# A chunked RWKV-7 recurrence on one NeuronCore: each chunk's map of the state worked out beside the inverse

## The chip, the core and the metric

The kernel runs on one core of a Trainium2 chip. The metric is device time in microseconds (us) of one execution, the median of some runs. PE is TensorE, DVE is VectorE, ACT is ScalarE, POOL is GpSimd, SP is SyncE, whose queue issues the DMAs here. Each engine works through its own instructions in order. L1550 means line 1550 of the kernel before; lines of the changed kernel are named as such.

## What is computed

One layer of a hybrid encoder: one projection of the normalised input, three mixers (A: RWKV-7, B: forgetting attention, C: sparse attention with a top-k), gates, and an output projection, for a prompt of 1024 rows and a sample of 64. The change concerns A, which has 8 heads of 64 columns and a state S of 64x64 per head:

```python
def step(S, inp):
    r_t, w_t, k_t, v_t, kk_t, a_t = inp
    sa = jnp.einsum('bhij,bhj->bhi', S, -kk_t)
    S = (S * w_t[:, :, None, :] + sa[..., None] * (kk_t * a_t)[:, :, None, :]
         + v_t[..., None] * k_t[:, :, None, :])
    return S, jnp.einsum('bhij,bhj->bhi', S, r_t)
wkv, y = lax.scan(step, wkv0, (tm(r), tm(decay), tm(k), tm(v), tm(kk), tm(a)))
```

## The kernel before

**Chunks, slots, units.** The 1024 rows are cut into 16 chunks of 64 rows, the sample is one more. Within a chunk the recurrence is solved in closed form, which needs the inverse of a triangular 64x64 matrix; from chunk to chunk only S is carried. A slot is one chunk of a pair of heads (the two heads h lie on partitions 0 to 63 and 64 to 127), a unit is four slots: 4 pairs x 4 units of the prompt, and the sample of all four pairs, 17 units and 68 slots.

**The steps of a unit**, each a generator that yields between its parts: `prepare` (L1271: `elem` loads wt, zt and QR and works out decays and scaled rows; `chunk_rows` makes the rows BA and the matrices BN and ND), `chunk_invert` (L1476: five doubling levels in float16, a correction, and the inverse UD), `value_rows` (L1411: turns values into UV and multiplies them by BN into P1), `chain` (below), and `tail` (L1586: norm, gate, store).

**The chain** (L1520) goes through the four slots of a unit one after the other. For each it multiplies S by QR (L1545), adds P1 into za (L1546), multiplies by the inverse UD (L1550), copies the result into UV (L1555), multiplies UV by BA for the new state (L1558, L1563), and by BA and S by QR for the output (L1567, L1569). Each of these waits for the one ahead:

```python
nc.tensor.matmul(pa[hv[h]], QR[hv[h], c, 1], S[hv[h]], ...)            # L1545
v.tensor_tensor(za, pa, P1[:, c], op=OP.add)                           # L1546
nc.tensor.matmul(pb[hv[h]], UD[hv[h], c], za[hv[h]], ...)              # L1550
v.tensor_copy(UV[hv[h], h, c], pb[hv[h]])                              # L1555
nc.tensor.matmul(ch[hv[h], ...], BA[:, h, c, 64 * h:64 * h + 64], UV[:, h, c], ...)   # L1558
v.scalar_tensor_tensor(self.state, ch[...], Pt[:, c, 64:65], sp, ...)  # L1563
```

**What sets the order.** `braid` lays the steps of several units side by side: in turn u, the tail of unit u-2, the chain of u-1, the inverse and value rows of u, and the preparation of u+1, each step at a fraction of the turn (step k of n stands at (k+0.5)/n, value rows at 0.4 of that); the top-k of mixer C runs along on DVE and ACT. After every step `pump` adds R_A/10 of a credit, and each whole credit issues one step of filler: three matmuls (L154) of the projections of the other mixers, 24 steps per 128 columns. What is left of the filler goes into the attention stage at other rates; after its last step the weights of the output projection take its place in SBUF, and then the output products (L1683) are the filler. Behind this a scheduler settles each engine's order from the program's order, priorities and when buffers come free.

**Buffers.** zt, P1, UV and UD have two buffers, QR and BA three, since the chain of u-1 still reads what the preparation of u+1 doubles. PSUM has eight banks: two for projections, one for turns, and the rings ga (one, preparation), gb (two, inverse), gc and gd (one each, chain).

## Time and profile before

| | |
|---|---|
| time, median of 3 runs | 1339.45 us (1335.56 to 1340.52) |
| profiled execution | 1332.74 us, its span 1331.0 us |
| PE busy | 1264.6 us, 95% of the span |
| DVE, ACT, POOL busy | 64%, 58%, 50% |
| mean granted clock of PE | 0.979 of 2.4 GHz |
| RWKV stage (L1398 and its like) | about 182 to 762 us |
| attention B and C, output | about 762 to 1331 us |

Busy times are shares of the span; PE's matmuls are pipelined and their ends are modelled, so what PE can do more is read from the waits and from the distance between starts. A matmul of float32 stands in the trace as two records.

### The profile page before, as it was taken

How to read it: one execution, taken by the hardware profiler on the slowest of the kernel's cores; microseconds unless marked ns; L12 is line 12 of the kernel's file. 1: busy time of each engine (PE TensorE's matmuls, PEld its weight loads, DVE VectorE, ACT ScalarE, POOL GpSimd, SP SyncE). 2: the span in 40 equal slices, each digit the busy share in tenths (PEclk: the TensorE clock that was granted, in tenths of full speed). 3: DMA queues.
4: the chain of work that ended last, by engine and by line, in shares of the span. 5: the costliest groups of instructions: out<-in, count | busy, mean ns of one | idle time of the engine just before them, and what ended most of it. 6: DMA issues, size and time to landing. Idle time of an engine off the chain costs nothing.

```text
span 1331.0 us, 29369 instructions
## 1 busy us (share of the span) xinstructions
PE 1264.6 (95%) x10563; PEld 963.3 (72%) x10563; DVE 847.0 (64%) x2483; ACT 776.7 (58%) x1758; POOL 667.7 (50%) x975
## 2 busy tenths in 40 slices
...
GB/s 224 71 109 67 133 82 98 62 62 94 63 70 110 95 80 127 136 94 111 101 104 112 117 215 250 219 193 216 189 171 157 145 206 182 145 116 108 92 75 96
DMA packets 172621, 169.60 MB, mean 127 GB/s; under 512 B 38546, under 2 KB 147130, under 8 KB 172475
## 3 DMA queue, kind: packets, MB, share of 16 engines
...
HBM read 104.61 MB, written 62.24 MB: 125 GB/s over the span
## 4 chain that ended last, share of the span: by engine, by line
PE 75%; DVE 9%; DMA 8%; ACT 4%; issue 2%; SPq 1%; POOL 1%; DVEq 0%; POOLq 0%; ACTq 0%
PE pproj L154 33%; PE pproj L1683 7%; PE ps_pv L980 5%; PE ps_atp L107 5%; PE ps_tp L1683 4%; PE ps_ga L1398 3%; PE ps_sc L949 2%; DMA wraw<-in_w_in_dram 2%; PE ps_sc L950 2%; PE ps_gb L1457 2%; PE ps_gb L1464 1%; PE ps_tp L107 1%; ACT junka L588 1%; PE ps_gc L1567 1%; PE ps_gc L1558 1%
## 5 line engine op out<-in xcount | busy, mean ns | idle before, releaser
L154 PE MATMUL pproj<-uH,wh 128*128 128x384 f32 (+4 forms) x1088 | 493.7, 454 | 0.0
L154 PE MATMUL pproj<-uH,wl 128*128 128x384 f32 (+4 forms) x1088 | 363.3, 334 | 0.0
L154 PE MATMUL pproj<-uL,wb 128*128 128x384 bf16 (+4 forms) x1088 | 358.7, 330 | 0.4 <-DVE zg L770 0.4
L154 PEld LDWEIGHTS pproj<-uH,wh 128*128 128x128 f32 (+1 forms) x1088 | 217.2, 200 | 3.5 <-issue 0.4
L154 PEld LDWEIGHTS pproj<-uH,wl 128*128 128x128 f32 (+1 forms) x1088 | 207.7, 191 | 2.2 <-issue 0.2
L154 PEld LDWEIGHTS <-wb 128*128 128x128 bf16 (+1 forms) x1088 | 106.3, 98 | 116.6 <-issue 79.7
L588 ACT ACTIVATE junka<-score,tk_tau 128x1024 f16<-128x1024 f32 (+4 forms) x160 | 149.3, 933 | 44.0 <-DVE tk_tau L602 26.5
L901 POOL TENSOR_SCALAR S<-S,mx 128x128 f32<-128x128 f32 (+8 forms) x136 | 105.3, 777 | 85.9 <-DVE mx L900 64.6
L140 POOL TENSOR_TENSOR wl<-wraw,wh 128x256 fp32r<-128x256 f32 (+1 forms) x184 | 138.4, 782 | 6.1 <-ACT wh L137 3.8
L919 DVE TENSOR_TENSOR hl<-ps_atp,hl 128x512 fp32r<-128x512 f32 (+3 forms) x184 | 109.1, 600 | 50.1 <-ACT hl L918 49.0
L896 ACT ACTIVATE S<-S,mx 128x128 f32<-128x128 f32 (+8 forms) x136 | 105.7, 778 | 47.0 <-DVE mx L892 42.3
L918 ACT CAST hl<-ps_atp 128x512 fp32r<-128x512 f32 (+3 forms) x184 | 93.0, 514 | 64.9 <-PE ps_atp L107 56.0
L142 POOL TENSOR_SCALAR wb<-wraw 128x512 bf16<-128x512 f32 (+1 forms) x92 | 62.5, 696 | 119.7 <-issue 50.2
L980 PE MATMUL ps_pv<-hl,VS 128*128 128x256 f32 (+3 forms) x640 | 113.1, 290 | 6.7 <-ACT hl L918 3.2
L107 PE MATMUL ps_atp<-ident,S 128*128 128x128 f32 x616 | 102.9, 278 | 1.0 <-DVE hl L919 0.9
L980 PEld LDWEIGHTS ps_pv<-hl,VS 128*128 128x128 f32 (+1 forms) x640 | 89.4, 175 | 19.6 <-ACT hl L918 4.5
L1146 POOL TENSOR_TENSOR cb<-nm,T 128x256 f32<-128x256 bf16 (+2 forms) x80 | 48.8, 616 | 63.3 <-DVE mx L892 46.9
L107 PEld LDWEIGHTS ps_atp<-ident,S 128*128 128x128 f32 x616 | 75.6, 143 | 6.0 <-POOL cb L1146 1.2
L1683 PE MATMUL pproj<-oh,gh 128*128 128x512 f32 x144 | 69.2, 501 | 0.7 <-ACT oh L1662 0.4
L137 ACT CAST wh<-wraw 128x1024 fp32r<-128x1024 f32 (+1 forms) x46 | 47.7, 1037 | 36.5 <-PE pproj L154 29.1
L790 DVE SCALAR_TENSOR_TENSOR zm<-pproj,omm,zs 128x384 f32<-128x384 f32 (+2 forms) x52 | 25.7, 494 | 45.9 <-ACT zs L789 42.6
L1683 PE MATMUL pproj<-ol,gb 128*128 128x512 bf16 (+1 forms) x144 | 52.9, 391 | 0.7 <-DVE ol L1663 0.7
...
## 6 DMA issues: line engine op xcount, KB each, us to landing
...
```

The costliest lines, as they stand in the source:

```text
L107: self.nc.tensor.transpose(out, x, self.ident[:n, :n])
L140: nc.gpsimd.tensor_tensor(l[:, k:k + 2, :n], raw[:, k:k + 2, :n], h[:, k:k + 2, :n], op=OP.subtract)
L142: nc.gpsimd.tensor_scalar(b[:, k:k + 4, :n], raw[:, k:k + 4, :n], 1.0, 0.0, op0=OP.mult, op1=OP.add)
L154: self.nc.tensor.matmul(ps[:n, :nt], a[:, k, :n], b[:, k, t0:t0 + nt], start=(k == 0 and i == 0), stop=(k == KD - 1 and i == 2))
L588: nc.scalar.activation(junk[:, :sc.shape[1]], sc, AF.Sign, bias=tf[:, j:j + 1], accum_out=cnt[:, j:j + 1])
L896: nc.scalar.activation(S[:, :kn], S[:, :kn], AF.Exp, bias=mx[:, nm - 1:nm], scale=-1.0, accum_out=mx[:, 6:7])
L901: nc.gpsimd.tensor_scalar(S[:, :kn], S[:, :kn], mx[:, 7:8], 0.5, op0=OP.mult, op1=OP.mult)
L918: nc.scalar.copy(ph[:kr, a:b], ps[:kr, a:b])
L919: nc.vector.tensor_tensor(pl[:kr, a:b], ps[:kr, a:b], ph[:kr, a:b], op=OP.subtract)
L980: nc.tensor.matmul(pv[0:m, q0:256], VS[:, kb, 0:m], hl[:, x, o:o + w], start=kb == 0 and x == 0, stop=at[-1][0] == last and n == 3)
L1146: nc.gpsimd.tensor_tensor(o, x, y, op=OP.add)
L1683: nc.tensor.matmul(ps[hf][:n, :], parts[m // 4][q][:, m % 4, :n], self.wo[m][q // 2][:, hf * 512:hf * 512 + 512], start=m == 0 and q == 0, ...
```

## The change

The chain's products are taken together. With the state S coming in, the new state is (I + W x B) S plus a constant, scaled by the decay, and the output is a product with S plus a constant; neither matrix nor constant needs S. A new generator `chunk_maps`, which runs at the end of `chunk_invert`, makes them for four slots at once: UD times QP (QP holds the turned rows of QR beside what was P1) gives W and UV; UV times BA gives the constants S0 and Y0; W times BA, plus the unit matrix and plus QR, gives the block matrices M. `chain` is then two products of M with S and one DVE operation per slot, and one addition of Y0 per unit. The turn's numbers of steps change with it (NCH 12 to 6, inverse 14 to 17), the chain's steps stand at 0.7 of the turn, and R_A is 7.5 instead of 7. QR has two buffers instead of three, BA two instead of three, zt, UV and UD one instead of two; M is one tile.

```diff
@@ braid
-        order = sorted(((k + 0.5) / n * (0.4 if work[j][0] == "rows" else 1), j) for j, (_, _, n) in enumerate(work) for k in range(n))
+        order = sorted(((k + 0.5) / n * dict(rows=0.4, chain=0.7).get(work[j][0], 1), j) for j, (_, _, n) in enumerate(work) for k in range(n))
@@ rwkv_pools
-        for t in self.ND:
+        self.M = one.tile([P, 2, 4, 2, 64], F32, name="M")
+        for t in self.ND + [self.M]:
@@ elem
-        zt = one.tile([P, 2, N], F32, tag="zt", name="zt", bufs=2)
-        QR = one.tile([P, 4, 3, 64], F32, tag="QR", name="QR", bufs=3)
+        zt = one.tile([P, 2, N], F32, tag="zt", name="zt")
+        QR = one.tile([P, 4, 3, 64], F32, tag="QR", name="QR", bufs=2)
@@ chunk_rows
-        BA = one.tile([P, 2, 4, 128], F32, tag="BA", name="BA", bufs=3)
+        BA = one.tile([P, 2, 4, 128], F32, tag="BA", name="BA", bufs=2)
@@ value_rows
-        P1 = one.tile([P, 4, 64], F32, tag="P1", name="P1", bufs=2)
-        UV = one.tile([P, 2, 4, 64], F32, tag="UV", name="UV", bufs=2)
+        QP = one.tile([P, 4, 2, 64], F32, tag="QP", name="QP")
+        UV = one.tile([P, 2, 4, 64], F32, tag="UV", name="UV")
-        x.update(P1=P1, UV=UV)
+        x.update(QP=QP, UV=UV)
+        sc.copy(QP[lo, :, 0], q2[lo, :, 0])
+        sc.copy(QP[hi, :, 0], q2[lo, :, 1])
...
-        sc.copy(P1, ps[:, :256].rearrange("p (c t) -> p c t", t=64))
+        sc.copy(QP[:, :, 1], ps[:, :256].rearrange("p (c t) -> p c t", t=64))
@@ chunk_invert, chunk_maps, chain
         v.tensor_tensor(R, bcast(con[:, C_I64:C_I64 + 64]), whole((ND[:, 0], T), (ND[:, 1], T), (eye, T)), op=OP.subtract)
         yield
-        UD = one.tile([P, 4, 64], F32, tag="UD", name="UD", bufs=2)
+        UD = one.tile([P, 4, 64], F32, tag="UD", name="UD")
         v.scalar_tensor_tensor(UD, U, -1.0, each(at(R), at(U)), op0=OP.mult, op1=OP.subtract)
-        x.update(UD=UD)
         yield
+        yield from self.chunk_maps(one, x, UD)
+    def chunk_maps(self, one, x, UD):
+        nc = self.nc
+        v, sc = nc.vector, nc.scalar
+        hv = (slice(0, 64), slice(64, 128))
+        QR, QP, BA, UV = x["QR"], x["QP"], x["BA"], x["UV"]
+        D = self.gring("gb", 2)
+        ps = D()
+        for c in range(4):
+            for h in range(2):
+                nc.tensor.matmul(ps[hv[h], c * P:c * P + P], UD[hv[h], c], QP[hv[h], c].rearrange("p a t -> p (a t)"), start=True, stop=True)
+        q = ps.rearrange("p (c a t) -> p c a t", a=2, t=64)
+        W = one.tile([P, 4, 64], F32, tag="W", name="W")
+        sc.copy(W, q[:, :, 0])
+        for h in range(2):
+            sc.copy(UV[hv[h], h], q[hv[h], :, 1])
+        yield
+        C = self.gring("gc", 1)
+        ch = C()
+        for a in range(2):
+            for c in range(4):
+                for h in range(2):
+                    e = h if a == 0 else 1 - h
+                    nc.tensor.matmul(ch[hv[e], 256 * a + c * 64:256 * a + c * 64 + 64], BA[:, h, c, 64 * e:64 * e + 64], UV[:, h, c],
+                                     start=True, stop=True)
+        S0, Y0 = [one.tile([P, 4, 64], F32, tag=n, name=n) for n in ("S0", "Y0")]
+        r3 = lambda t: t.rearrange("p (c t) -> p c t", t=64)
+        v.tensor_tensor(S0, r3(ch[:, 0:256]), x["Pt"][:, :, 64:65].broadcast_to([P, 4, 64]), op=OP.mult)
+        sc.copy(Y0, r3(ch[:, 256:512]))
+        x.update(S0=S0, Y0=Y0)
+        yield
+        ps = D()
+        for c in range(4):
+            for h in range(2):
+                nc.tensor.matmul(ps[hv[h], c * P:c * P + P], W[hv[h], c], BA[hv[h], h, c], start=True, stop=True)
+        q = ps.rearrange("p (c a t) -> p c a t", a=2, t=64)
+        M = self.M
+        i64 = self.con[:, C_I64:C_I64 + 64].rearrange("p (o t) -> p o t", o=1).broadcast_to([P, 4, 64])
+        for h in range(2):
+            v.tensor_tensor(M[hv[h], 0, :, h], q[hv[h], :, h], i64[hv[h]], op=OP.add)
+            v.tensor_tensor(M[hv[h], 1, :, 1 - h], q[hv[h], :, 1 - h], QR[hv[h], :, 0], op=OP.add)
+        yield
+        x.update(M=M)
     def chain(self, one, slots, x):
-        G = self.gring("gc", 1)
         hv = (slice(0, 64), slice(64, 128))
-        i64 = self.con[:, C_I64:C_I64 + 64]
-        QR, UD, P1, BA, UV, Pt = x["QR"], x["UD"], x["P1"], x["BA"], x["UV"], x["Pt"]
+        M, Pt, S0, Y0 = self.M, x["Pt"], x["S0"], x["Y0"]
+        ch = self.gring("gd", 1)()
+        flat = lambda t: t.rearrange("p h t -> p (h t)")
         sample = slots[0][1] == 16
         s0 = x.get("s0")
-        if sample:
-            send = one.tile([P, 256], F32, tag="e1", name="s_end").rearrange("p (c t) -> p c t", t=64)
         Yt = one.tile([P, 4, 64], F32, tag="Yt", name="Yt", bufs=2)
+        ST = one.tile([P, 4, 64], F32, tag="ST", name="ST", bufs=2)
         ends = []
-        ch, ab = G(), self.gring("gd", 1)()
         for c, (hp, t) in enumerate(slots):
             S = s0[:, hp] if sample else self.state
             if t == 0:
-                S = one.tile([P, 64], F32, tag="S", name="S", bufs=2)
+                S = one.tile([P, 64], F32, tag="S", name="S")
                 v.memset(S, 0.0)
-            za, sp = [one.tile([P, 64], F32, tag=n, name=n) for n in ("za", "sp")]
-            pa, pb = [ab[:, 256 * i + c * 64:256 * i + c * 64 + 64] for i in range(2)]
-            for h in range(2):
-                nc.tensor.matmul(pa[hv[h]], QR[hv[h], c, 1], S[hv[h]], start=True, stop=True)
-            v.tensor_tensor(za, pa, P1[:, c], op=OP.add)
-            sc.activation(sp, S, AF.Copy, scale=Pt[:, c, 64:65])
-            yield
-            for h in range(2):
-                nc.tensor.matmul(pb[hv[h]], UD[hv[h], c], za[hv[h]], start=True, stop=True)
-            for h in range(2):
-                if UA >> h & 1:
-                    sc.copy(UV[hv[h], h, c], pb[hv[h]])
-                else:
-                    v.tensor_copy(UV[hv[h], h, c], pb[hv[h]])
-            yield
-            for h in range(2):
-                nc.tensor.matmul(ch[hv[h], c * 64:c * 64 + 64], BA[:, h, c, 64 * h:64 * h + 64], UV[:, h, c], start=True, stop=True)
-            if sample:
-                self.state = send[:, c]
-            else:
-                self.state = one.tile([P, 64], F32, tag="S", name="S", bufs=2)
-            v.scalar_tensor_tensor(self.state, ch[:, c * 64:c * 64 + 64], Pt[:, c, 64:65], sp, op0=OP.mult, op1=OP.add)
-            py = ch[:, 256 + c * 64:320 + c * 64]
-            for h in range(2):
-                nc.tensor.matmul(py[hv[1 - h]], BA[:, h, c, 64 - 64 * h:128 - 64 * h], UV[:, h, c], start=True, stop=False)
-            for h in range(2):
-                nc.tensor.matmul(py[hv[1 - h]], QR[hv[h], c, 0], S[hv[h]], start=False, stop=True)
+            nc.tensor.matmul(ch[:, c * 64:c * 64 + 64], flat(M[:, 0, c]), S, start=True, stop=True)
+            nc.tensor.matmul(ch[:, 256 + c * 64:320 + c * 64], flat(M[:, 1, c]), S, start=True, stop=True)
+            self.state = ST[:, c]
+            v.scalar_tensor_tensor(self.state, ch[:, c * 64:c * 64 + 64], Pt[:, c, 64:65], S0[:, c], op0=OP.mult, op1=OP.add)
             if t >= 15:
                 ends.append((hp, self.state))
             yield
-        sc.copy(Yt, ch[:, 256:512].rearrange("p (c t) -> p c t", t=64))
+        v.tensor_tensor(Yt, ch[:, 256:512].rearrange("p (c t) -> p c t", t=64), Y0, op=OP.add)
+        yield
         if ends:
             ps = self.tp()
-            so = one.tile([64, n, P], F32, tag="QR" if sample else "so", name="so", bufs=3 if sample else 1)
+            so = one.tile([64, n, P], F32, tag="QR" if sample else "so", name="so", bufs=2 if sample else 1)
@@ program
-                work.append(("invert", s.chunk_invert(s.one, x[u]), 14, ()))
+                work.append(("invert", s.chunk_invert(s.one, x[u]), 17, ()))
@@ numbers
-NCH=12
+NCH=6
-R_IDX, R_A, R_FOX, R_DSA1, N_TOPK,LATE = (70,5.5),7,1.56,2.32,17,1000
+R_IDX, R_A, R_FOX, R_DSA1, N_TOPK,LATE = (70,5.5),7.5,1.56,2.32,17,1000
```

**PE, one slot of the chain, in the kernel before** (ps_gd and ps_gc are PSUM tiles of the chain, kc and arn belong to other work, U_5481 to the next unit's inverse):

```order
L154 MATMUL pproj<-uH,wl 128x384
L107 MATMUL ps_tp<-ident,kc 128x128 x4
L1567 MATMUL ps_gc<-UV,BA 64x64 x2
L1569 MATMUL ps_gc<-S,QR 64x64 x2
L1545 MATMUL ps_gd<-S,QR 64x64 x2
L1457 LDWEIGHTS U_5481
```

The last of three visits of a slot; L1550 and L1558 stand apart, ahead of it, with filler between. **The same engine, one slot in the changed kernel:**

```order
L154 MATMUL pproj<-uH,wl 128x384
L1589 MATMUL ps_gd<-ST,M 128x64
L1590 MATMUL ps_gd<-ST,M 128x64
L1351 MATMUL ps_ga<-ident,arn 64x128 x4
L1461 LDWEIGHTS U_5812
```

Three visits with ten products have become one with two. In the stage 95 visits of the old chain follow directly on an L154 row; of the new blocks with half the array (L1535, L1549, L1561) 34 do, and 52 of L1589.

**PE, the end of a unit's inverse, before** (directly behind the last product that makes UD and the eight turns L1471 of the next unit's U):

```order
L1471 MATMUL ps_gb<-identh,U_5821 64x64
L154 LDWEIGHTS wb
L154 MATMUL pproj<-uL,wb 128x384
L1279 MATMUL ps_ga<-wt,wabh 128x256
L1280 MATMUL ps_ga<-wt,wabl 128x256
```

**And in the changed kernel**, between that product and the same turns (now L1475):

```order
L1535 MATMUL ps_gb<-QP,UD 64x128 x8
L154 LDWEIGHTS wb
L154 MATMUL pproj<-uL,wb 128x384
L154 MATMUL pproj<-uH,wh 128x384
L154 MATMUL pproj<-uH,wl 128x384
L1561 MATMUL ps_gb<-BA,W 64x128 x8
L1549 MATMUL ps_gc<-UV,BA 64x64 x16
L1475 LDWEIGHTS U_5812
```

The three new blocks stand here, with one step of filler between the first and the second; in four of 17 units there is none. On DVE the four additions into M follow UD at once:

```order
L1521 SCALAR_TENSOR_TENSOR UD<-U_9636,ps_gb 128x256
L1566 TENSOR_TENSOR M<-ps_gb,con 64x4x64
L1567 TENSOR_TENSOR M<-ps_gb,QR 64x4x64
L1566 TENSOR_TENSOR M<-ps_gb,con 64x4x64
L1567 TENSOR_TENSOR M<-ps_gb,QR 64x4x64
L720 TENSOR_TENSOR kcs<-ps_tp,kcs 128x512
L1362 TENSOR_TENSOR QR<-zt,Pt 128x4x64
L1553 TENSOR_TENSOR S_9752<-ps_gc,Pt 128x256
L1592 SCALAR_TENSOR_TENSOR ST<-ps_gd,Pt,S_9752 128x64
```

Before, the same stretch of DVE's queue held the chain's L1546, L1555 and L1563, four times per unit among other work:

```order
L1555 COPY UV<-ps_gd 64x64 x2
L1607 TENSOR_TENSOR Yt<-Yt,gst 128x256
L641 TENSOR_SCALAR eq,tk_need<-sg 128x1024
L1495 TENSOR_TENSOR Y_8826<-ps_gb,con 128x256
L1353 SCALAR_TENSOR_TENSOR QR<-zt,par,ps_ga 128x4x64
L1563 SCALAR_TENSOR_TENSOR S<-ps_gc,Pt,sp 128x64
```

So a unit has four DVE answers for the chain instead of twelve, and two bursts at its end. Over the program, 1923 L154 rows stand between the first and the last PE row of the RWKV stage before, 1770 after. The last L154 row stands behind the 110th L949 row (a score of attention) before and behind the 122nd after, the first output product behind the 125th and the 129th.

## Rows read from the trace of the kernel before

**Rows 1.** The page's first part: busy us, share of the span, instructions.

```profile
PE 1264.6 (95%) x10563; PEld 963.3 (72%) x10563; DVE 847.0 (64%) x2483; ACT 776.7 (58%) x1758; POOL 667.7 (50%) x975
```

**Rows 2.** Stretches: length, busy time of PE, PEld, DVE, ACT, POOL, clock, DMA.

```profile
182.00:762.00 580.00, 560.29 (x6316) 420.30 (x6314) 418.35 (x1290) 366.86 (x852) 296.12 (x453) 0.98 0.31 94
762.00:1062.80 300.80, 293.43 (x1984) 247.55 (x1984) 161.47 (x524) 181.94 (x434) 185.97 (x295) 0.99 0.70 196
1062.80:1089.00 26.20, 18.20 (x102) 14.65 (x101) 21.33 (x77) 19.51 (x47) 16.07 (x26) 0.86 0.73 201
```

**Rows 3.** What PE waited for, 182 to 762 us: total, times, longest.

```profile
PE ps_gb L1457 <- DVE Y L1495: 2.6, 3, 1.6
...
PE ps_gc L1558 <- DVE UV L1555: 1.8, 3, 0.8
...
PE ps_gb L1464 <- DVE T L1500: 1.5, 2, 1.1
...
PE ps_gc L1567 <- DVE S L1563: 0.9, 3, 0.4
```

**Rows 4.** PE in time: start, us, instruction, records, idle before and releaser.

```profile
399.95 0.34 PE L154 MATMUL pproj<-uH,wl 128*128 128x384 f32 x1
400.13 0.34 PE L154 MATMUL pproj<-uL,wb 128*128 128x384 bf16 x1
...
408.61 0.34 PE L154 MATMUL pproj<-uH,wl 128*128 128x384 f32 x1
408.88 0.33 PE L1550 MATMUL ps_gd<-za,UD 64*64 64x64 f32 x4
409.53 0.33 PE L1558 MATMUL ps_gc<-UV,BA 128*64 128x64 f32 x2 [0.32 <-DVE UV L1555]
409.79 0.29 PE L1464 MATMUL ps_gb<-T,ND 128*128 128x64 f16 x4
...
413.20 0.34 PE L1567 MATMUL ps_gc<-UV,BA 128*64 128x64 f32 x4
...
413.74 0.34 PE L154 MATMUL pproj<-uL,wb 128*128 128x384 bf16 x1
```

**Rows 5.** PE in time, at the rows nearest to the new products.

```profile
415.69 0.67 PE L1443 MATMUL ps_ga<-UV,BN 64*64 64x64 f32 x14
416.30 0.29 PE L1464 MATMUL ps_gb<-T,ND 128*128 128x64 f16 x4
...
425.19 1.15 PE L1398 MATMUL ps_ga<-QR,BK 64*128 64x128 f32 x8
...
494.32 0.31 PE L154 MATMUL pproj<-uH,wl 128*128 128x320 f32 x1
494.46 0.50 PE L1317 MATMUL ps_ga<-ones,k 128*128 128x2 f32 x4
494.82 0.30 PE L154 MATMUL pproj<-uL,wb 128*128 128x320 bf16 x1
```

**Rows 6.** DVE and ACT groups, 182 to 762 us: busy, mean ns, idle before.

```profile
L1555 DVE COPY UV<-ps_gd 64x64 f32<-64x64 f32 x136 | 29.8, 219 | 24.0 <-PE ps_gd L1550 21.3
L1563 DVE SCALAR_TENSOR_TENSOR S<-ps_gc,Pt,sp 128x64 f32<-128x64 f32 x64 | 17.9, 279 | 14.9 <-PE ps_gc L1558 13.5 <-ACT qh L692 0.5 <-ACT T L1509 0.5
L1402 DVE TENSOR_TENSOR BN<-ps_ga,con 128x256 f32<-128x256 f32 x34 | 14.3, 422 | 16.8 <-PE ps_ga L1398 16.6
...
L588 ACT ACTIVATE junka<-score,tk_tau 128x1024 f16<-128x1024 f32 x31 | 35.6, 1147 | 28.9 <-DVE tk_tau L602 26.5 <-DVE tk_tau L598 2.1
...
L1444 ACT COPY P<-ps_ga 128x256 f32<-128x256 f32 x17 | 6.2, 365 | 11.4 <-PE ps_ga L1443 10.2 <-PE ps_gb L1457 1.1
```

**Rows 7.** What the SP queue waited for, 150 to 780 us: total, times, longest.

```profile
SPq L1304 <- PE ps_gd L1545: 100.4, 11, 18.5
```

**Rows 8.** PE in time, the last projection and the first output product.

```profile
1062.64 0.31 PE L154 MATMUL pproj<-uH,wl 128*128 128x320 f32 x1
...
1089.04 1.20 PE L1683 MATMUL pproj<-oh,gh 128*128 128x512 f32 x2
```

## The prediction

> **What bounds the kernel now.** I read the page's first part, then the stretches, then what TensorE (PE) waited for, then PE's rows in order of time. The reader should see in the first that PE is busy 95% of the span [rows 1], and in the second that this holds stage by stage: 560 of 580 us in the RWKV stage, 293 of 301 us in the attention that follows, and one stretch, 1062.8 to 1089.0 us, where it is busy only 18.2 of 26.2 us at a mean granted clock of 0.86 [rows 2]. DVE and ACT are busy 418 and 367 of the 580 us. So PE bounds nearly everything, and the projections (L154) are what fills it: wherever they stand they cost the same. An edit pays in three ways only: fewer PE-microseconds, fewer PE waits, or filler put where PE lacks it.
>
> **PE work taken out.** A slot of the old chain visits PE three times. From start to start L1558 takes 0.26 us (409.53 to 409.79), L1550 about the same (0.33 with the pipeline's tail), and L1567, L1569 and L1545 together 0.54 (413.20 to 413.74) [rows 4]. That is 1.07 us, for 68 slots 73 us. Besides, L154 is followed by its like after 0.18 us (399.95 to 400.13) but by L1550 after 0.27 (408.61 to 408.88) [rows 4]: 0.09 us for the change from the whole array to its halves. In the order of before 95 visits of the chain stand directly behind an L154 row: 8.5 us. Out: **82 us**.
>
> **PE work put in.** L1535 and L1561 are 16 records each per unit, 64x64 blocks with 128 columns, the two halves h side by side. The nearest rows are L1443 (halves side by side, 64 columns: 14 records in 0.61 us) and L1398 (one half at a time, 128 columns: 8 records, 1.15 us with the tail) [rows 5]. Eight pairs of 128 columns should last as long as eight single ones, some 1.1 us each; if the halves did not overlap, 2.2. I take 1.1, since L1443 is the same use of the array. L1549 is 32 records of 64 columns in pairs: twice L1443, 1.2 us. The new chain has two products per slot with 128 rows and 128 columns of weights, four records; the nearest row is L1317, four records with 128x128 weights in float32, 0.36 us from L154 to L154 (494.46 to 494.82) [rows 5], with two columns moving instead of 64. I take 0.37; the bound from above is 0.54, the slot's longest old visit. Per unit 1.1 + 1.1 + 1.2 + 4 x 0.37 = 4.9 us, for 17 units 83 us; 34 of the new blocks stand behind L154 and pay the 0.09 (3 us), L1589 doesn't, as L1317 doesn't. In: 86 us, bounds 80 and 98 (without overlap 123, which L1443 excludes). I take 84, since L1549 mostly follows L1561 at once and shares its tail. **Net +2 us**, -2 to +16.
>
> The Trainium skill, TensorEngine Tiling (Array Packing), Theoretical Speedup, speaks against the new chain: with contraction and columns of 64 or less, packing the array is said to gain up to two times, and a block matrix of 128x128 that is half zeros gives that up. By that rule, packed products would make the chain 68 x 0.18 = 12 us cheaper than I count. The rows here show no such gain for blocks this short: eight packed records by L1443 are 0.35 us, four whole ones by L1317 0.36. The same page's Key Properties say that a change of tiling mode drains the engine, which agrees with the 0.09 us above.
>
> **Work beside PE.** DVE loses 16 short operations per unit (8 L1555, 4 L1563, and 4 L1546 that I price like L1555: 12 x 0.219 + 4 x 0.279 = 3.7 us) and gains 4 of L1563's kind, four adds into M (0.22 to 0.42 each) and S0 and Yt (0.42 by L1402): 2.8 to 3.6 us. ACT loses four sp scalings and the Yt copy and gains six copies of 0.365 us like L1444 [rows 6]: under 1 us more of 34 per unit. POOL gets one memset. None of these bounds, so I put them at nothing; what covers them is PE's own 34 us per unit.
>
> **Buffers and SP.** zt, QR, BA, UV and UD have one buffer less. A load of QR already waits for PE's last reading of an older QR, 100.4 us in 11 waits of the SP queue [rows 7], with wt, zt and weight loads queued behind it, and PE does not wait for any of them. Now it waits for the adds into M at the end of the unit before, which is about as late. zt waits for the same unit's elementwise part instead of the one before; that part comes in the first third of a unit of 34 us, which leaves over 20 us. I put both at nothing; if a load came late, PE would wait once a unit, 17 times.
>
> **PE waits taken out.** L1558 1.8 and L1567 0.9 us [rows 3], with some smaller ones of the chain, 1 us by guess: **-4 us**, between -3 and -6.
>
> **PE waits put in.** UD was needed much later; now L1535 follows it, then W (an ACT copy) and L1561, then M and L1589. A return trip with little between shows at 408.88: L1550 starts, DVE copies, L1558 starts 0.65 us later after 0.32 us idle [rows 4]. In the order of the change the filler between L1535 and L1561 is mostly one step of three L154 rows, 0.53 us, and none in four of 17 units. With ACT free that nearly covers a copy of 0.365 us; behind one of the top-k's activations of up to 1.15 us [rows 6] it doesn't. The inversion's own trips are thinner too: fewer steps stand between them, and 41 of its 204 trips have under 0.65 us of other PE rows between, where 9 had. What such a trip costs is bounded by zero (DVE and ACT early) and by the 4.1 us that L1457 and L1464 wait for DVE in 5 waits [rows 3], 0.8 each. I take 0.2 us for each new trip behind L1535 and UD (17 units) and 0.1 for the 32 thin ones, near the lower end, because most of the cover is still there: 3.4 + 3.2, **+6 us**, bounds 0 and 25.
>
> **Filler moved.** A unit has fewer steps (39 calls instead of 43 at 0.75 instead of 0.7), and the end of the stage too; the order has 1770 L154 rows in the RWKV stage instead of 1923. 153 rows, 27 us of PE, go to the attention. Both places are full, so the move itself costs nothing. But the last L154 now stands behind the 122nd L949 score instead of the 110th, and the first output product (L1683) behind the 129th instead of the 125th. In the trace that bare stretch runs from 1062.64 to 1089.04 [rows 8]: 8.0 us idle, and 0.14 x 2 x 26.2 = 7.3 us at the lower level of 1.2 GHz, which lose 3.7 more: 11.7 us. Seven scores of 15 remain bare: 5.5 us lost, **-6 us**, between 0 and -12.
>
> **The sum.** +2 - 4 + 6 - 6 = -2 us against the profiled execution's 1332.74 us (its span is 1331.0). That lies 6.7 us under the median of 1339.45, so I carry the difference over: **1337 us**. No change, within what can be told: 0.5%, 6.7 us, is about what a measurement of this kernel tells from none.
>
> **Rivals.** (1) *The new trips are hidden and the stage's queues run smoother.* For: the chain held DVE, in order, behind PE for three answers per slot, and now for one; PE's waits for L1457 and L1464 come from a late DVE. Against: thinner cover. Then the +6 falls away and the 4.1 us of those waits too, with half of the lost clock in the stage (mean clock 0.98 [rows 2]: about 12 us lost, 6 back): 1337 - 16 = 1321; I give it 1325, three quarters of that. (2) *ACT answers late, slower.* W and UV stand in ACT's queue behind activations of about 1 us, and L1561 stands in PE's queue with everything behind it. Each late answer idles PE, and after idle PE the clock falls to 1.2 GHz. From a mean of 0.9 us per unit on, the new trips eat all gains; with 20 us instead of 6: 1351. (3) *The bare stretch doesn't shrink*: if the loading of w_out after the last projection takes its 26 us whatever runs, the -6 falls away: 1343, no change. That the chain keeps its length is excluded by the order, which has two products and one DVE step per slot.
>
> **Chances.** Forecast 0.40 (its own range 1331 to 1344), rival 1 0.30, rival 2 0.20, rival 3 0.10. Faster by over 0.5% (below 1332.75): 0.30 and a fifth of the forecast, 0.38. Slower (above 1346.1): 0.20 and a little, 0.22. The rest, 0.40, is within. The range takes most of the rivals in: 1321 to 1351.
>
> **What would show it.** Right: L1589 and L1590 together near 0.37 us per slot, L1535 and L1561 near 1.1; waits of PE at L1561 and L1535 of a few us in all; the bare stretch under 18 us. Wrong: halves that don't overlap in L1535 (2.2 us), L1561 waiting for W over 15 us in all, more stretches at 1.2 GHz in the stage, or PE waiting for zt.

## The result: slower by 3.8%, and the profile after

The changed kernel takes 1386.17 us (1383.46 to 1388.1), against 1337.51 us of the kernel before in the same runs: a ratio of 1.0382, interval 1.0357 to 1.0408. That is 49 us, outside the forecast range and beyond the rival that named the right kind of loss (1351). The first part of the page shows nothing dramatic, as the answer to [rows 1]: PE 93% instead of 95%.

The page's first part, changed kernel (busy us, share of the span, instructions):

```profile
PE 1280.5 (93%) x10545; PEld 1002.7 (73%) x10563; DVE 839.6 (61%) x2381; ACT 788.0 (57%) x1775; POOL 667.3 (48%) x976
```

PE is busy 16 us longer and the span is 50.7 us longer, so two thirds of the loss are time in which PE does nothing. Where, the stretches say. Two of them are the same in any version: from the first row product (L1398, after L1400) to the first score of attention (L949), here called the stage, and from there to the last product. A third takes ten whole turns out of the stage, from the value products (L1443, after L1447) of the second unit to those of the twelfth, before the top-k ends.

Stretches of the kernel before (stage, what follows, ten units): length, busy time of PE, PEld, DVE, ACT and POOL, mean granted clock, DMA share, GB/s:

```profile
182.20:790.60 608.40, 588.05 (x6489) 441.18 (x6488) 420.81 (x1294) 378.69 (x878) 316.00 (x483) 0.98 0.33 99
790.60:1323.80 533.20, 516.34 (x3167) 405.14 (x3167) 323.85 (x953) 313.81 (x713) 274.39 (x389) 0.98 0.58 163
229.50:543.40 313.90, 305.18 (x3593) 229.79 (x3592) 241.33 (x775) 245.47 (x563) 159.11 (x246) 0.99 0.29 89
```

The same three of the changed kernel:

```profile
182.00:829.60 647.60, 590.25 (x6410) 464.65 (x6409) 415.48 (x1191) 387.00 (x891) 308.88 (x476) 0.97 0.30 91
829.60:1374.50 544.90, 528.33 (x3231) 418.78 (x3249) 321.65 (x953) 316.66 (x717) 280.11 (x397) 0.98 0.57 163
234.60:593.20 358.60, 325.35 (x3613) 257.14 (x3612) 242.53 (x735) 258.90 (x585) 157.51 (x250) 0.95 0.26 78
```

Length less PE's busy time is PE's idle time: in the stage 20.4 us before and 57.4 after, in what follows 16.9 and 16.6, in the ten units 8.7 and 33.2. So the new idle time lies in the RWKV stage, two thirds of it in ordinary units, 3.3 us each instead of 0.9. DVE and ACT have hardly more to do than before: 415 and 387 us of 648, where it was 421 and 379 of 608.

An account of the stage: its L154 rows at 0.18 us each [rows 4], PE's idle time, half of the time at 1.2 GHz, and what is left over, which is PE's other work. Before: 1810 rows make 325.8, idle 20.4, and of the granted clock 23.9 us stand at the lower level, 12.0 lost; left over 250. After: 1734 rows 312.1, idle 57.4, 41.0 us at the lower level, 20.5 lost; left over 258. The stage is longer by 37.0 of idle time, 8.5 of clock and 7.4 of work (the product rows alone give 7, see below), and shorter by 13.7 of filler, together 39.2. What follows gets the filler back (75 rows, 13.5 us) and is 11.7 us longer. In all 51 us.

What PE waited for in the ten units (total, times, longest), in the kernel before, the two largest rows of 8 us in all:

```profile
PE ps_ga L1407 <- DVE BA L1402: 2.5, 1, 2.5
PE ps_gc L1558 <- DVE UV L1555: 1.1, 2, 0.8
```

And in the changed kernel, the five largest of 32 us in all:

```profile
PE ps_gb L1468 <- ACT T L1513: 5.9, 6, 1.8
PE ps_ga L1409 <- DVE BA L1404: 4.6, 2, 3.9
PE ps_gb L1461 <- DVE Y L1499: 4.2, 6, 1.9
PE ps_ga L107 <- DVE ass L1324: 3.7, 2, 3.0
PE ps_gb L1561 <- ACT W L1538: 3.0, 6, 0.8
```

Only the last is a new instruction. The rest are old steps, of the inverse (answers to [rows 3]) and of the preparation, which now come late. The new trip itself looks like this; all engines in time, changed kernel, at one L1561 (start, us, engine, instruction, idle before and releaser):

```profile
295.50 1.09 PE L1535 MATMUL ps_gb<-QP,UD 64*64 64x128 f32 x16
295.95 0.19 ACT L588 ACTIVATION_READ_ACCUMULATOR junka<-score,tk_tau 128x1 f32 x1
296.17 0.83 ACT L588 ACTIVATE junka<-score,tk_tau 128x640 f16<-128x640 f32 x1
296.90 0.19 ACT L588 ACTIVATION_READ_ACCUMULATOR junka<-score,tk_tau 128x1 f32 x1
297.00 0.35 ACT L1538 COPY W<-ps_gb 128x256 f32<-128x256 f32 x1
297.40 0.87 PE L1561 MATMUL ps_gb<-BA,W 64*64 64x128 f32 x11 [0.81 <-ACT W L1538]
```

The copy of W takes 0.35 us, but stands behind an activation of the top-k of 0.83. And the same at an old step, the turn of U for the inverse's last correction:

```profile
461.48 0.31 PE L1475 MATMUL ps_gb<-identh,U 64*64 64x64 f16 x8
...
462.06 1.03 ACT L588 ACTIVATE junka<-score,tk_tau 128x896 f16<-128x896 f32 x1
463.00 0.19 ACT L588 ACTIVATION_READ_ACCUMULATOR junka<-score,tk_tau 128x1 f32 x1
463.09 0.47 ACT L692 ACTIVATE kT<-pproj 128x384 f32<-128x384 f32 x1
463.46 0.47 ACT L692 ACTIVATE kh<-pproj 128x384 fp32r<-128x384 f32 x1
463.83 0.36 ACT L1513 COPY T<-ps_gb 128x256 f16<-128x256 f16 x1
464.25 0.22 PE L1468 MATMUL ps_gb<-T,ND 128*128 128x64 f16 x2 [1.84 <-ACT T L1513]
```

Ahead of the copy stand an activation of the top-k and two copies that park projections, that is, work that the filler itself brings to ACT. In the stage I count 61 waits of PE of 0.25 us and more for DVE, ACT or POOL, 50 us in all, where the kernel before has 29 and 18 us; in 47 of the 61 (19 of the 29) the late engine had come to the answer straight from other work, with a pause of 0.02 us at most. DVE's answers make 28 of the 50 us and ACT's 21, where before they made 15 and 2. Behind one such wait the clock is down: PE idles 2.98 us up to 251.87 (for L1324), and from 250.7 to 257.5 the granted clock stands at 1.2 GHz.

### The profile page after: what moved, and what is told of

Same layout as the page of the kernel before. It is cut to its first block, busy times and chain, and to the rows that moved or that the text cites. A ratio compares the mean times of both kernels' runs of the same rounds, so it can differ in the third digit from the quotient of the medians.

```text
span 1381.7 us, 29248 instructions
## 1 busy us (share of the span) xinstructions
PE 1280.5 (93%) x10545; PEld 1002.7 (73%) x10563; DVE 839.6 (61%) x2381; ACT 788.0 (57%) x1775; POOL 667.3 (48%) x976
## 4 chain that ended last, share of the span: by engine, by line
PE 67%; DVE 11%; DMA 7%; ACT 6%; POOL 4%; issue 3%; SPq 2%; POOLq 0%; DVEq 0%; ACTq 0%
PE pproj L154 28%; PE pproj L1707 7%; PE ps_pv L980 5%; PE ps_atp L107 4%; PE ps_tp L1707 4%; PE ps_sc L949 2%; PE ps_sc L950 2%; PE ps_ga L1400 2%; DMA wraw<-in_w_in_dram 2%; ACT junka L588 2%; PE ps_gb L1461 2%; SPq L840 1%; PE ps_gc L1549 1%; PE ps_gb L1561 1%; POOL wl L140 1%
## 5 line engine op out<-in xcount | busy, mean ns | idle before, releaser
L154 PE MATMUL pproj<-uH,wh 128*128 128x384 f32 (+4 forms) x1088 | 501.9, 461 | 0.0
L154 PE MATMUL pproj<-uH,wl 128*128 128x384 f32 (+4 forms) x1088 | 366.6, 337 | 0.0
L154 PE MATMUL pproj<-uL,wb 128*128 128x384 bf16 (+4 forms) x1088 | 362.7, 333 | 3.3 <-ACT kh L692 1.7
L154 PEld LDWEIGHTS pproj<-uH,wh 128*128 128x128 f32 (+1 forms) x1088 | 220.4, 203 | 7.6 <-issue 4.1
L154 PEld LDWEIGHTS pproj<-uH,wl 128*128 128x128 f32 (+1 forms) x1088 | 211.2, 194 | 2.7 <-issue 0.9
L154 PEld LDWEIGHTS <-wb 128*128 128x128 bf16 (+1 forms) x1088 | 108.9, 100 | 114.6 <-issue 82.9
L588 ACT ACTIVATE junka<-score,tk_tau 128x1024 f16<-128x1024 f32 (+4 forms) x160 | 149.5, 934 | 50.5 <-DVE junk L582 31.2
L896 ACT ACTIVATE S<-S,mx 128x128 f32<-128x128 f32 (+8 forms) x136 | 105.7, 777 | 46.8 <-DVE mx L892 43.1
L107 PE MATMUL ps_atp<-ident,S 128*128 128x128 f32 x616 | 100.7, 276 | 2.9 <-DVE hl L919 2.9
L980 PEld LDWEIGHTS ps_pv<-hl,VS 128*128 128x128 f32 (+1 forms) x640 | 90.1, 175 | 13.5 <-DVE hl L919 2.1
L107 PEld LDWEIGHTS ps_atp<-ident,S 128*128 128x128 f32 x616 | 75.2, 142 | 8.1 <-issue 3.6
L137 ACT CAST wh<-wraw 128x1024 fp32r<-128x1024 f32 (+1 forms) x46 | 47.8, 1040 | 44.0 <-PE pproj L154 37.1
L1707 PE MATMUL pproj<-ol,gb 128*128 128x512 bf16 (+1 forms) x132 | 48.8, 390 | 1.2 <-DVE ol L1687 0.9
```

What stands on the lines that cost most here:

```text
L107: self.nc.tensor.transpose(out, x, self.ident[:n, :n])
L154: self.nc.tensor.matmul(ps[:n, :nt], a[:, k, :n], b[:, k, t0:t0 + nt], start=(k == 0 and i == 0), stop=(k == KD - 1 and i == 2))
L588: nc.scalar.activation(junk[:, :sc.shape[1]], sc, AF.Sign, bias=tf[:, j:j + 1], accum_out=cnt[:, j:j + 1])
L896: nc.scalar.activation(S[:, :kn], S[:, :kn], AF.Exp, bias=mx[:, nm - 1:nm], scale=-1.0, accum_out=mx[:, 6:7])
L980: nc.tensor.matmul(pv[0:m, q0:256], VS[:, kb, 0:m], hl[:, x, o:o + w], start=kb == 0 and x == 0, stop=at[-1][0] == last and n == 3)
L1707: nc.tensor.matmul(ps[hf][:n, :], parts[m // 4][q][:, m % 4, :n], self.wo[m][q // 2][:, hf * 512:hf * 512 + 512], start=m == 0 and q == 0, ...
```

## The experiments

All times are medians; ratios are against the kernel before measured together with it. Idle times are worked out as above from the stretches of one profiled execution of each. Two of these stand apart from their medians: a_wdve's (1370.1 us) is its fastest, a_nomaps_cover's (1365.9) its slowest.

| kernel | us | ratio (interval) | L154 in stage | idle, stage | idle, ten units |
|---|---|---|---|---|---|
| before | 1337.5 | | 1810 | 20.4 | 8.7 |
| changed | 1386.2 | 1.0382 (1.0357 to 1.0408) | 1734 | 57.4 | 33.2 |
| a_spread | 1378.2 | 1.0320 (1.0278 to 1.0363) | 1734 | 57.9 | 31.5 |
| a_wdve | 1377.4 | 1.0309 (1.0263 to 1.0355) | 1734 | 51.5 | 24.9 |
| a_notrip | 1367.2 | 1.0232 (1.0208 to 1.0257) | 1734 | 40.3 | 19.7 |
| a_later | 1361.5 | 1.0187 (1.0153 to 1.0222) | 1713 | 44.5 | 20.1 |
| a_later8 | 1357.2 | 1.0156 (1.0136 to 1.0177) | 1827 | 33.7 | 15.1 |
| a_later8_rg16 | 1360.1 | 1.0174 (1.0143 to 1.0205) | 1827 | 37.5 | 16.1 |
| a_split | 1383.6 | 1.0367 (1.0334 to 1.0400) | 1788 | 51.9 | 20.2 |
| a_rate9 | 1396.1 | 1.0443 (1.0406 to 1.0480) | 2032 | 43.1 | 22.4 |
| a_rate7 | 1418.1 | 1.0591 (1.0565 to 1.0616) | 1619 | 71.4 | 32.4 |
| a_bufs | 1381.6 | 1.0330 (1.0303 to 1.0356) | 1734 | 56.5 | 32.9 |
| a_qr3 | 1390.6 | 1.0385 (1.0356 to 1.0413) | 1734 | 62.5 | 30.6 |
| a_nomaps | 1305.4 | 0.9764 (0.9731 to 0.9798) | 1624 | 51.0 | 16.2 |
| a_nomaps_cover | 1358.0 | 1.0171 (1.0119 to 1.0223) | 1844 | 39.5 | 12.8 |
| b_bunch | 1350.0 | 1.0106 (1.0078 to 1.0133) | 1810 | 29.2 | 15.5 |
| b_rate62 | 1341.1 | 1.0042 (1.0023 to 1.0062) | 1611 | 33.8 | 10.6 |
| b_rate72 | 1363.8 | 1.0193 (1.0166 to 1.0219) | 1837 | 33.6 | 5.0 |
| b_rate72_rg15 | 1364.0 | 1.0204 (1.0174 to 1.0235) | 1837 | 33.3 | 4.8 |
| b_rg17 | 1335.7 | 0.9998 (0.9980 to 1.0016) | 1810 | 24.3 | 8.7 |

The theories: **A1**, the old chain's visits to PE were what covered the inverse's trips, and without them the trips lie bare. **A2**, the new trips bring the idle time, since they are dependent steps more in the same turn, each behind busy queues. Beside them the single numbers and buffers of the change.

### Freeing and moving the maps

**a_notrip**: the same products and copies, but the products read data that is ready.

```diff
-                nc.tensor.matmul(..., W[hv[h], c], BA[hv[h], h, c], start=True, stop=True)
+                nc.tensor.matmul(..., UD[hv[h], c], BA[hv[h], h, c], start=True, stop=True)
-                    nc.tensor.matmul(..., BA[:, h, c, 64 * e:64 * e + 64], UV[:, h, c],
+                    nc.tensor.matmul(..., BA[:, h, c, 64 * e:64 * e + 64], QP[:, c, h],
```

> The changed kernel with the new products freed of their answers: L1561 multiplies by UD instead of W, and L1549 by QP instead of UV, so neither waits for ACT; every product and copy is still made, only what the two read is other data. Theory A2 (the trips through ACT inside the maps cost): PE's waits at L1561 (4.0 us, and 7.8 of its weight load) vanish, the idle time of the stage goes from 57 to 45 or less and the time to 1370 or less. Theory A1 (cover lost elsewhere): idle 50 or more, time within 8 us of the changed kernel's.

1367 us, 19 us less than the changed kernel; idle time 40.3 instead of 57.4. Stage and ten units:

```profile
182.20:811.70 629.50, 589.19 (x6410) 462.09 (x6409) 416.08 (x1191) 388.16 (x891) 312.03 (x477) 0.99 0.31 94
236.00:571.70 335.70, 316.03 (x3609) 249.35 (x3608) 243.66 (x729) 255.94 (x580) 160.17 (x248) 0.99 0.28 83
```

ACT, DVE and POOL do what they did in the changed kernel (388, 416 and 312 us), so what goes away is the price of the dependence, not of the load. In the ten units 13.5 of 24.5 us of new idle time go, and the clock is back at 0.99 there. Waits at L1561 were 4.0 us in the stage and yet 17 us of idle time vanish: what comes late at the end of an inverse makes other steps late as well. In the ten units L1409's 4.6 us go to nothing, L1461's fall from 4.4 to 2.3. The three largest rows that are left:

```profile
PE ps_gb L1468 <- ACT T L1513: 5.3, 6, 1.5
PE ps_gb L1535 <- DVE UD L1521: 3.8, 5, 1.7
PE ps_gb L1461 <- DVE Y L1499: 2.0, 4, 0.7
```

Two of them did not fall. For L1468 PE waits 6.9 us in all, 6.6 in the changed kernel and 1.7 (as L1464) before, and for L1535 3.8 instead of 1.3. So the dependence of L1549 and L1561 on ACT carries over half of the new idle time of the ten units, and 19 of the 49 us; the rest stays while the maps stand at the end of the inverse, waiting or not.

**a_later**: the maps as a part of their own at the head of the next turn, ahead of the chain; the inverse has 14 steps again. **a_later8**: the same with R_A 8.

```diff
-        order = sorted(((k + 0.5) / n * dict(rows=0.4, chain=0.7).get(work[j][0], 1), j) for ...)
+        at = dict(rows=(0.2, 0.3), maps=(0, 0.3), chain=(0.3, 0.65))
+        order = sorted((at.get(work[j][0], (0, 1))[0] + (k + 0.5) / n * at.get(work[j][0], (0, 1))[1], j) for ...)
-        yield from self.chunk_maps(one, x, UD)
+        x.update(UD=UD)
...
+                work.append(("maps", s.chunk_maps(s.one, x[u - 1]), 3, ()))
-                work.append(("invert", s.chunk_invert(s.one, x[u]), 17, ()))
+                work.append(("invert", s.chunk_invert(s.one, x[u]), 14, ()))
```

> The changed kernel with the three map products taken out of the inverse's sequence (14 steps again) and put as a part of their own at the head of the next unit's turn, ahead of the chain; value rows in the middle of the turn, QR with three and UD with two buffers. The products are the same. Theory A (the inverse has become 17 dependent trips in a turn of the same PE work, and each has less between): the waits at L1461 and L1468 go back from 17 us to near the 6 us of before, the time to 1345 to 1360. Rival C (what costs is ACT and DVE, which have the new copies and additions to do wherever they stand): within 8 us of 1386.

> The version that makes the maps one turn later (1361 us), with the filler rate 8 instead of 7.5, so that the stage holds about as many L154 rows as in the kernel before (1810; 1713 at 7.5). Theory A (cover): idle time of the stage 44 to 36 or less, the stage longer by 97 rows x 0.18 = 17 us less that, and the end 4 to 10 us earlier, 1351 to 1357. Rival: the stretch after the last projection grows by as much as the stage gains, as at rate 9, and the time stays within 4 us of 1361.

1361.5 and 1357.2 us, 1.5 and 0.2 us past what A gave: the new place gives back 25 us (the value rows and the chain moved in the turn with the maps; the buffers for QR and UD do nothing, as a_qr3 shows below), and about the filler of before another 4. The waits at L1461 and L1468 fall from 18 to 10 us in a_later's stage, not to 6. Ten units of a_later8:

```profile
239.40:576.40 337.00, 321.89 (x3644) 254.17 (x3644) 245.60 (x737) 259.87 (x589) 168.79 (x258) 0.99 0.29 88
```

15.1 us idle, with the full new work in it. a_later8 is the best version with maps that ran; it is still 1.6% behind the kernel before.

**a_wdve**: `sc.copy(W, ...)` becomes `v.tensor_copy(W, ...)`.

> The changed kernel with one copy moved: W is copied out of PSUM by DVE instead of ACT. If late answers of ACT behind the top-k's activations are a large part of the loss, the waits at L1561 halve and the time falls by 4 us or more; if DVE is as late as ACT, within 3 us of the changed kernel's.

1377.4 us, about 9 less, with executions from 1370 to 1385: in the ten units 24.9 us idle instead of 33.2. But the waits at L1561 did not halve: 2.3 us instead of 3.0 in the ten units, 5.9 instead of 4.0 in the stage. The copy takes 0.42 us on DVE and 0.37 on ACT. So the gain is not the one meant, and it is no larger than what a_spread's shift of the chain gives below; which queue the answer should stand in is not shown.

### What the old chain covered

**a_nomaps**: the generator of the maps is not called; the chain multiplies by tiles that are zeroed once.

```diff
-        yield from self.chunk_maps(one, x, UD)
...
-        M, Pt, S0, Y0 = self.M, x["Pt"], x["S0"], x["Y0"]
+        M, Pt, S0, Y0 = self.M, x["Pt"], self.S0, self.Y0
```

> The changed kernel without its new generator: the three blocks of products L1535, L1549 and L1561, their copies and the additions into M are left out, the inverse has 14 steps, and the chain multiplies by tiles that are filled once. PE loses 57 us of work. From the first row product to the first score of attention PE was idle 20 us in the kernel before, 57 in the changed one. Theory A1 (the old chain's visits were what stood between the trips of the inverse, and without them the trips lie bare): idle stays at 40 us or more, the time comes down by little more than the 57 us, to 1325 to 1340. Theory A2 (the new trips and answers themselves, at the end of the inverse, bring the idle time): idle falls to 15 to 28 us, the time to 1285 to 1300.

**a_nomaps_cover**: in addition three visits of two independent 64x64 products per slot, at the old chain's places, with before's step numbers and rate.

```diff
+            visit(2)
+            yield
+            visit(2)
+            yield
+            visit(2)
             nc.tensor.matmul(ch[:, c * 64:c * 64 + 64], flat(M[:, 0, c]), S, start=True, stop=True)
```

> The changed kernel without the maps (their products, copies and additions left out, the chain on tiles filled once), and with three more visits of two 64x64 products per slot, at the three places of a slot at which the old chain visited PE; these products wait for nothing, and nobody reads them. Steps of the chain, its position and the filler rate are those of the kernel before. PE has about the work of the kernel before. Theory A1 (the old chain's visits, although each waited for the one ahead, were what PE did while the inverse's answers came): the idle time of the stage falls from the 51 us of the version without maps to 28 us or less, and the time is at or below the kernel before's, 1318 to 1336. Rival (buffers, QP's copies or another part of the change that stands in both): idle time 40 us or more, 1345 or more.

Read by the stage, neither theory wins. a_nomaps has 51.0 us idle, as A1 wanted, but 1305.4 us, near A2's time and below A1's. a_nomaps_cover has 39.5 and 1358.0 us, against A1; its rival (another part of the change, which stands in both) has its time and misses its idle time by 0.5 us. The stretches part the two halves of the stage. The ten units of a_nomaps, and the ten units and the rest of the stage of a_nomaps_cover:

```profile
239.70:503.70 264.00, 247.78 (x2713) 196.26 (x2713) 201.00 (x609) 209.84 (x470) 133.36 (x215) 0.99 0.28 83
...
243.50:557.60 314.10, 301.35 (x3421) 239.33 (x3417) 214.91 (x653) 237.11 (x521) 151.72 (x239) 0.97 0.30 90
557.60:809.90 252.30, 225.60 (x2108) 175.61 (x2107) 131.83 (x345) 98.36 (x232) 134.77 (x204) 0.95 0.37 114
```

In the ten units the maps' absence takes 17.0 of the 24.5 us (33.2 to 16.2), and the visits, with the position, steps and rate of before, take 3.4 more. So there A2 carries some two thirds and A1 a small part at most. The rest of the stage is another matter: 26.7 us idle and a clock of 0.95 in a_nomaps_cover behind 557.6, where the kernel before has 9.5 and 0.97:

```profile
543.40:790.60 247.20, 237.69 (x2457) 177.39 (x2456) 149.93 (x429) 105.20 (x254) 132.82 (x197) 0.97 0.38 116
```

There the top-k ends and the units run out, and a_nomaps_cover, with about PE's work of before and no map at all, is 23 us slower than the kernel before. Why is not settled.

**a_split**: a_later8 with each block of products in four parts, with other work between, rate 6.5.

```diff
                 nc.tensor.matmul(..., UD[hv[h], c], QP[hv[h], c]..., start=True, stop=True)
+            if c < 3:
+                yield
```

> The version that makes the maps one turn later at filler rate 8 (1357 us, 33.7 us idle in the stage), with the same products in twelve steps instead of three: after each slot's part of L1535, L1549 and L1561 other work may stand. Copies and additions stay whole, and the rate is 6.5, for the same filler per turn. Theory A1 (it matters how finely PE's work stands between the trips): idle time 25 us or less, 1345 to 1351. Rival (the work on PE and the late answers of ACT and DVE set it, whatever the grain): within 5 us of 1357.

1383.6 us, 26 us worse than a_later8, with 20.2 us idle in the ten units and 31.7 outside them. Both expectations miss. A finer grain did not cover more here, but the run does not part this from two other things: a block in twelve steps ends later in the turn, and the rate shifts the order of everything (b_rate72 below).

### Numbers and buffers

**a_spread**: the chain at factor 1 instead of 0.7. **b_bunch**: the old chain at 0.7.

> The changed kernel with one number undone: the chain's steps are spread over the whole turn again (position factor 1 instead of 0.7), everything else as changed. Theory A (the twelve short chain steps that used to stand between the inverse's trips are gone, and three new trips came in; where the six that are left stand matters little): within 6 us of the changed kernel's 1386, waits of PE in the RWKV stage near 45 us as in the changed kernel's trace. Rival B (the last third of each turn has been left without chain steps, and the trips there lost their cover): 1360 or less, PE's waits at L1461 and L1468 halved.

> The kernel before with one number of the change: the old chain's steps stand in the first 0.7 of each turn. Theory A1: the last third of each turn's inverse loses its cover, the idle time of the stage goes from 20 to 27 to 35 us and the time up by 6 to 15 us, 1342 to 1350. Rival: the position doesn't matter, within 4 us of the kernel before.

The position costs the kernel before 14 us (1.0106; ten units 15.5 us idle instead of 8.7, the stage 29.2), as A1 said: where the old chain stood did cover something. In the changed kernel it costs 8 by the medians, 2 more than A allowed, and in the stage nearly all of it is clock: idle time is the same, but 20 us of the stage stand at the lower level instead of 41. Rival B, with 1360 and half the waits, falls.

**a_rate9**, **a_rate7**, **b_rate62**, **b_rate72**: R_A 9 and 7 in the changed kernel, 6.2 and 7.2 in the one before.

> The changed kernel with more filler per step in the RWKV stage (rate 9 instead of 7.5, so 0.9 of a filler step behind every step instead of 0.75). Theory A (cover between trips is what is missing): PE's waits in the RWKV stage fall by a third, 15 us; the stage gets longer by the filler it takes over, and the end comes 8 to 15 us earlier, 1371 to 1378. Rival C (late answers of ACT and DVE behind the top-k, whatever cover): no change by more than 6 us.

> The changed kernel with the filler rate of before, 7 instead of 7.5. If what stands between the trips decides: 4 to 8 us more idle time in the stage than the changed kernel's 57, the stage shorter by its filler, and the time 1386 to 1396. If the rate doesn't matter: within 4 us of 1386.

> The kernel before with less filler per step in the RWKV stage (rate 6.2 instead of 7), so that about as much filler is left for the attention stage as in the changed kernel, with the old chain. Theory A: cover per step is down by 11%, the waits of the stage rise from 18 us by 5 to 10, and the time to 1343 to 1352. Rival D (moving filler into the attention is itself what costs, by the shift of the last projection behind more scores): 1365 or more, with the loss behind the RWKV stage.

> The kernel before at filler rate 7.2 instead of 7: a shift of the steps' order and nothing else. If the order of before merely fits its numbers, any shift costs: 3 to 10 us more than the kernel before, as rate 6.2 (6.5 us). If it doesn't: within 3 us of the kernel before.

More filler per step does cover, though the times came out otherwise than expected: from rate 7 over 7.5 to 9 the ten units' idle time is 32.4, 33.2, 22.4 and the stage's 71.4, 57.4, 43.1. But at rate 9 the projections are used up before the attention needs them, and between the last L154 and the first output product PE idles and slows, for the 84 us of the next row (1396 us where 1371 to 1378 was expected):

```profile
1053.20:1137.10 83.90, 62.75 (x313) 52.23 (x312) 51.40 (x181) 48.02 (x126) 45.67 (x82) 0.69 0.60 163
```

At rate 7 the idle time grows by 14 us, but the time by 32, beyond both expectations: the stage stands at a mean clock of 0.95, and what follows has 115 L154 rows more. b_rate62 moves 201 rows out of the stage of the kernel before. Its stage idles 13 us more, 2 of them in the ten units, but behind it idle time stays at 17.3 us (16.9), and the time rises by 6 us: D falls, the moved filler costs nothing there beyond its own work.

The largest surprise is b_rate72. Ten units of it, the rest of its stage and what follows:

```profile
235.10:548.10 313.00, 308.02 (x3614) 232.08 (x3614) 236.84 (x777) 248.07 (x568) 160.79 (x253) 1.00 0.30 91
548.10:803.40 255.30, 231.33 (x2446) 172.80 (x2445) 147.27 (x427) 103.91 (x255) 135.51 (x199) 0.98 0.36 110
803.40:1354.10 550.70, 524.08 (x3138) 409.33 (x3138) 322.73 (x953) 309.84 (x705) 271.95 (x382) 0.96 0.56 158
```

A rate 3% higher, nothing else, makes the kernel before 26 us slower, beyond both expectations. Its ten units are better than ever (5.0 us idle at full clock); it loses 24.0 us to idle at the end of the stage, where before lost 9.5, and 26.6 us behind it, with a clock of 0.96, where before lost 16.9 at 0.98. That is the scale by which order alone moves this kernel, and about half of the change's whole loss.

**b_rg17** (RG 1.7 instead of 2.1, the rate of the last projections), **b_rate72_rg15**, **a_later8_rg16**: the filler ends later, the RWKV stage is as it was.

> The kernel before with the rate of the last projections in the attention 1.7 instead of 2.1. The stretch between the last projection and the first output product (26.4 us, 11.7 lost in it) shrinks below 18 us; by the prediction's term that is worth 4 to 8 us, 1328 to 1333. If filler that stands thinner in the attention loses as much elsewhere: within 3 us of the kernel before.

> The kernel before at RWKV filler rate 7.2 (1364 us), with the rate of the last projections in the attention 1.5 instead of 2.1, so that they end some ten scores later. If the bare stretch behind the last projection carries that version's loss: 1342 to 1352, the stretch under 30 us instead of 49. If the RWKV stage carries it: within 5 us of 1364.

> The version that makes the maps one turn later, at RWKV rate 8 (1357 us, a bare stretch of 35 us), with the rate of the last projections in the attention 1.6 instead of 2.1: the stretch under 20 us, the time 1347 to 1352. What is then left against the kernel before is 6 us of products and the idle time of the stage, 33.7 us instead of 20.

The stretch between the last projection and the first output shrinks as meant: 26.4 to 15.5 us, 49.0 to 18.1, 34.9 to 17.8. The time does not: 0.9998 (0.9980 to 1.0016) for the first, 1364.0 and 1360.1 us against 1363.8 and 1357.2 for the others. In b_rg17 the loss in the stretch itself falls from 11.7 to 6.2 us, as meant, but behind the stage PE idles 18.6 us in all, where it was 16.9: the loss moves to another place.

**a_bufs**: zt and UV with two buffers. **a_qr3**: QR with three, UD with two.

> The changed kernel with two buffers again for zt and UV, nothing else. If the thinner buffers cost nothing, as the prediction said: within 6 us of the changed kernel's 1386, idle time of the stage 50 us or more. If they are behind the rest of the idle time: 1378 or less, idle time under 45 us.

> The changed kernel with three buffers again for QR and two for UD, nothing else. As predicted (no cost): within 6 us of 1386. If the load of QR, which now waits for the additions into M, makes the preparation late: 1378 or less, and the SP queue's 57.6 us of waiting for M gone.

Idle times 56.5 and 62.5 us in the stage, 32.9 and 30.6 in the ten units: these buffers carry nothing of it. a_bufs is 5 us faster by the median, with as much idle time and less time at the lower clock (51 us in the stage and behind it, where it was 61). BA was not given back, and QP's two copies were not tried apart; their part stays open.

## Why the prediction was wrong, point by point

**What bounds.** PE does, in both kernels; that no row of its waits came to more than 2.6 us [rows 3], and so nothing was to fear, was true of the order that the kernel before has, not of the kernel.

**PE work out and in: too small as a net, inside its bounds.** From start to start, waits of 0.15 us and more taken out, the old chain's rows take 78.6 us in the trace of before and the new ones 85.8. (The forecast's 82 and 84 hold 8.5 and 3 us for the change to half the array; that time falls in the L154 rows ahead and is not in these sums.) PE in time, changed kernel, at the new products:

```profile
413.76 0.41 PE L1589 MATMUL ps_gd<-ST,M 128*128 128x64 f32 x2
414.01 0.39 PE L1590 MATMUL ps_gd<-ST,M 128*128 128x64 f32 x2
414.24 0.61 PE L107 MATMUL ps_ga<-ident,BK 128*128 128x128 f32 x4
...
504.39 1.09 PE L1535 MATMUL ps_gb<-QP,UD 64*64 64x128 f32 x16 [0.52 <-DVE UD L1521]
505.41 0.31 PE L154 MATMUL pproj<-uL,wb 128*128 128x320 bf16 x1
...
507.01 1.09 PE L1561 MATMUL ps_gb<-BA,W 64*64 64x128 f32 x16 [0.47 <-ACT W L1538]
508.03 0.31 PE L154 MATMUL pproj<-uL,wb 128*128 128x320 bf16 x1
```

L1535 and L1561 take 1.02 us (1.1 forecast; the two halves do run side by side), the slot's two products 0.48 at 413.76 and as the median of all slots where they stand together, where L1317 had promised 0.37. Net +7 instead of +2, bounds -2 and 16. The short chain saves PE no work.

The Trainium skill (TensorEngine Tiling (Array Packing), Theoretical Speedup) gives packed small products a gain of up to two. The trace agrees at 128 columns: sixteen records of L1535 in 1.02 us, against eight of single products of L1398 in 1.15 with their tail [rows 5]. I had denied the gain for the chain by L1317, which moves two columns and not 64: four whole records take 0.48 us and not 0.36, eight packed ones of L1443 0.35 [rows 5]. By these rows a packed chain would take 0.13 us less per slot, 9 us in all, before its changes of mode; this is an estimate, and no such chain was run.

**PE waits put in: the step that failed.** I counted trips with little cover and gave each 0.1 to 0.2 us, "near the lower end, because most of the cover is still there": +6, bounds 0 and 25. (The 3.4 in it is one trip a unit, where the sentence names two.) The stage has 37 us more idle time, and 8.5 more lost to the clock. Two things were wrong in it. I priced a late answer by its copy, and in the rows shown it costs what stands ahead of it in the late engine's queue: 0.81 us at 297.40, behind L588, and 1.84 at 464.25, behind L588 and L692. And I priced each trip alone. Freed of waiting, the maps give back 17 us of idle time though PE had waited only 4.0 us at L1561 itself; much of the rest was at L1409, L1400, L107 and L1461, old steps of the same turn. What a_notrip leaves in the ten units over the kernel before is mostly at L1468 and L1535. That part went only when the maps left the inverse (a_later8, ten units: 2.8 us at L1468's like, none at L1535's). Why L1468's answer from ACT is late there, though the map products wait for nothing, is not shown.

Of the signs that I had set, "L1561 waiting for W over 15 us in all" looked at the wrong line: L1561 and L1535 waited 6.0 us together, the few us that were to show me right, beside a loss of 49. "More stretches at 1.2 GHz in the stage" did come.

**PE waits taken out: -4, right in part.** The old waits at L1558 and L1567 are gone, but L1589 now waits 2.3 us for the state (L1592).

**Bare stretch: -6, wrong.** It shrank as forecast, from 26.4 to 15.8 us (1130.95 to 1146.71). But the loss in it did not shrink with its length: 8.9 us instead of 11.7 (4.6 idle, and half of 8.5 at the lower level), where 5.5 was forecast. And it was worth nothing: idle time behind the stage is 16.9 and 16.6 us, and b_rg17 makes the same shrinkage in the kernel before for 0.9998. I had taken a place where time is lost for a cause of the loss.

**Filler moved: right.** Between the first and the last PE row of the RWKV stage 153 rows fewer, as the order said; up to the first score, which ends the stage here, 76 fewer, and 75 more behind it. That the move costs nothing behind the stage, b_rate62 shows too. **Buffers: right for zt and QR**, as a_bufs and a_qr3 show (UV and UD with them); BA was not tried.

**Rivals.** The second, ACT answers late and the clock falls, is nearest to what happened, at twice its price and more: 20 us of new trips were named for it, 45 were measured with the clock. It had 0.20. But the trip that it named, L1561, waited 4.0 us, and DVE's late answers cost more than ACT's (28 and 21 us). Its threshold was a slip: by the forecast's own sum 8 us, 0.5 per unit and not 0.9, eat all gains. The first (1325) had nothing in it: DVE, whose chain answers fell from twelve to four per unit, answered later, not earlier (28 us of waits for it, 15 before).

**How much is the change and how much the order.** In the ten units five versions with the maps inside the inverse and the copy on ACT have 30.6 to 33.2 us idle, whatever rate from 7 to 7.5, position and buffers they have; six with the old chain have 4.8 to 15.5. That difference, some 20 us, belongs to the change. So does where the maps stand: the waits of the inverse's own trips (L1461 and L1468 or their like) in the ten units are 8.7 to 21.0 us in the eight versions with the maps inside the inverse, 5.8 to 7.9 in the four with them a turn later, 2.6 and 4.6 in the two without, and 0.4 to 3.6 in the six with the old chain. What the clock adds there is not tied to the idle time: 34 us at the lower level in the changed kernel, 7 to 31 in the other four of the five, 7 before. At the end of the stage it is otherwise. Outside the ten units the stage idles 24 us instead of 12, and there the shifts of the filler rate cost the kernel before as much (23 in b_rate62, 29 in b_rate72). How the 49 us would come out at the best numbers for each kernel stays open; the best version with maps that ran is 21 us behind.
